# Moving PSUM evacuations and low parts between VectorE, ScalarE and GpSimd in a two-layer diffusion backbone

## Chip, cores and metric

The kernel runs on one core of a Trainium2 chip. The metric is the device time of one execution in microseconds (us); the time given for a kernel is the median of its runs. All times below are us unless marked ns.

## Reference

Two layers of a hybrid backbone work on 512 latent tokens with a prefix of 256 context tokens, 1024 channels wide. Each layer normalises and modulates its input, makes one combined input projection, runs three branches on slices of it (latent attention, a multi-scale pooling mixer, and a bidirectional gated linear attention, GLA), gates and merges them and adds the result to its input:

```python
def trunk_layer(x, xc, mod, mod_c, ...):
    shift, scale, gate = jnp.split(mod[:, None, :], 3, axis=-1)
    z = split_columns((rmsnorm(x, pre_g) * (1 + scale) + shift) @ w_in)
    zc = split_columns((rmsnorm(xc, pre_g) * (1 + scale_c) + shift_c) @ w_in)
    y_mla, yc_mla = mla_branch(z, zc, ...)
    y_pool = pool_branch(z, pool_w, pool_scale)
    y_gla, yc_gla = gla_branch(z, zc, ...)
    out = merge_branches(z, y_mla, y_pool, y_gla, w_bm, w_bp, w_bg, w_out)
    x = x + gate * rmsnorm(out, post_g)
    ...   # the same for the context xc, in the first layer only
```

The GLA runs over chunks of tokens in both directions. Its keys `k` (256 columns of `z`) and values `v` (512 columns) are the two that the change speaks of, and its decays are `log_sigmoid(...) / 16`.

## The kernel before

**Number format.** Everything is float32, and a product of two float32 matrices is made of three TensorE products of rounded parts: `split` (L76 to 78) makes a high part on ScalarE and a low part, value minus high part, on VectorE unless told otherwise; `mm3` (L91 to 94) issues high times high, high times low, low times high.

**Tiles.** The 768 tokens are six tiles `t` of 128: 0 and 1 are context, 2 to 5 the latents. A layer's input is held transposed in two SBUF tensors, `hh` and `hl` (high and low part), as eight blocks `k` of 128 channels by 768 tokens. `z_A` (L304) multiplies a block of weights with it so that the output channels lie on partitions (the keys `gk`, two blocks, each 512 latents and then 256 context tokens); `z_B` (L316) makes tokens by channels (the values `gv`, two weight halves `i` of 256 channels, six tiles each). Their PSUM results leave by way of a staging tile (pool `stage`, two buffers a tag) and a GpSimd DMA to DRAM, from where the GLA scan reads them.

**Who empties PSUM.** `stage_out` (L330 to 339) empties `gk`, `gq` and others, all on ScalarE. `rows_block` (L412 to 418) empties one `gv` tile after another, on ScalarE too; each of the two buffers of PSUM pool `psz` (tag "z") holds one tile of `gv`, so tile t+2 can't be started before tile t has left:

```python
            ps = z_B(blk, w0, w, hT, t, name)
            st = stage.tile([P, w], F32, tag="st", name=f"st_{name}_{t}")
            with urgent():
                act(st, ps)
```

**The input of the second layer.** `emit_hT` (L1099 to 1111) makes it at the end of the first, for two tiles of tokens at a time (three calls of eight blocks, 24 steps). In a step TensorE transposes a block into a PSUM tile `xT` (pool `pst`, tag "t", two buffers); the affine `hv = xT * scale + shift` empties it on VectorE (L1108); ScalarE makes the high part; GpSimd makes the low part, `hl = hv - hh` (L1111, listed at the helper's line, L71). Around it the first layer's output rows `xo` and residuals `xres` are made on VectorE (L74, L294), and the second layer's first weights are split (`wh_gq` on ScalarE, `wl_gq`, `wl_ak` on VectorE).

**The GLA's gates.** `forget(c)` makes the decay of two tiles: matmuls `pre`, then on ScalarE Abs, Exp and Ln, then on VectorE four operations `e <- pre, e`, then Exp on ScalarE. The scan of tile c (`gla_tile`) is a long row of small VectorE multiplications on `pfx`, `sfx` and `tot` with TensorE products `lv` of the operands `pqk` between.

**What sets the order.** No order is written out by hand: the program is built under a scheduler that simulates a time line and puts each engine's instructions in a queue of its own, with `urgent()` raising the priority of what it encloses. Each engine then works through its queue in that order. So an edit of a few lines also moves rows that it doesn't touch.

Of the kernel before, what the change touches and what calls it, by code (L numbers as in the profile page):

```python
# [11 lines left out]
F32 = mybir.dt.float32  # L12
F32R = mybir.dt.float32r
U32 = mybir.dt.uint32
AF = mybir.ActivationFunctionType
ALU = mybir.AluOpType
# [32 lines left out]
def hybrid_kernel(ctx, tc, io, out):  # L49
    nc = tc.nc  # L50
    V, S, G, PE = nc.vector, nc.scalar, nc.gpsimd, nc.tensor

    def opened(name, bufs=2, side=None, space=None):
        kw = {} if space is None else {"space": space}
        return tc.tile_pool(name=name, bufs=bufs, side=side, reuse_waits="tile", **kw)
# [11 lines left out]
    def act(out, in_, func=AF.Copy, **kw):  # L67
        return S.activation(out=out, in_=in_, func=func, **kw)  # L68

    def tt(out, a, b, op=ALU.mult, eng=None):  # L70
        return (eng or V).tensor_tensor(out=out, in0=a, in1=b, op=op)  # L71
# [37 lines left out]
    def urgent(key="x"):  # L109
        return tc.high_priority(offset=offs.get(key, URGENT)) if offs.get(key, URGENT) else nullcontext()  # L110

    def load_split(src, nk, width, name, pool=stream):
        raw = load_raw(src, nk, width, name, pool)
        h = pool.tile([P, nk, width], F32R, tag="wh", name=f"wh_{name}")
        l = pool.tile([P, nk, width], F32R, tag="wl", name=f"wl_{name}")
        with urgent("split"):
            split(h, l, raw)
        return h, l
# [158 lines left out]
    def dtile(shape, name, dt=F32):  # L277
        return dram.tile(shape, dt, name=name)
# [4 lines left out]
    def new_hT(l, pool):  # L283
        return (pool.tile([P, KD, T], F32R, name=f"hh{l}", bufs=1),
                pool.tile([P, KD, T], F32R, name=f"hl{l}", bufs=1))
# [18 lines left out]
    def z_A(blk, hT, with_ctx, name, psum=None, tag="z"):  # L304

        wh, wl = blk
        res = []
        for t0, n in ((CTX, LAT),) + (((0, CTX),) if with_ctx else ()):
            ps = (psum or psz).tile([P, n], F32, tag=tag, name=f"zA_{name}_{t0}")
            for k in range(KD):  # L310
                mm3(ps, wh[:, k, :], wl[:, k, :], hT[0][:, k, t0:t0 + n], hT[1][:, k, t0:t0 + n],
                    k == 0, k == KD - 1)
            res.append((ps, t0, n))
        return res

    def z_B(blk, c0, w, hT, t, name, psum=None, tag="z"):  # L316

        ps = (psum or psz).tile([P, w], F32, tag=tag, name=f"zB_{name}_{t}")
        ts = slice(t * P, t * P + P)
        kb = KD // len(blk)  # L320
        for k in range(KD):
            wh, wl = blk[k // kb]
            mm3(ps, hT[0][:, k, ts], hT[1][:, k, ts], wh[:, k % kb, c0:c0 + w], wl[:, k % kb, c0:c0 + w],
                k == 0, k == KD - 1)
        return ps

    def wblock(l, name, i):
        return load_split(io["w_in"][l, BLOCK_START[name] + i], KD, P, f"{name}{i}_{l}")

    def stage_out(parts, dst, name, scale=None):  # L330

        st = stage.tile([P, T], F32, tag="st", name=f"st_{name}")
        for ps, t0, n in parts:
            if scale is None:
                act(st[:, t0:t0 + n], ps)
            else:
                act(st[:, t0:t0 + n], ps, scale=scale)
        lo = min(p[1] for p in parts)
        nc.gpsimd.dma_start(out=dst[:, lo:T], in_=st[:, lo:T])
# [17 lines left out]
    def layer(l, hT, close_hT, side, todo_mod):  # L357
# [5 lines left out]
        zqk = dtile([8, 64, T], f"zqk{l}")  # L363
# [48 lines left out]
        def rows_block(blk, w0, w, dst, c0, tiles, name):  # L412
            for t in tiles:
                ps = z_B(blk, w0, w, hT, t, name)
                st = stage.tile([P, w], F32, tag="st", name=f"st_{name}_{t}")
                with urgent():
                    act(st, ps)
                nc.gpsimd.dma_start(out=dst[t * P:t * P + P, c0:c0 + w], in_=st)


# [4 lines left out]
        def z_gq():  # L425
            for c in range(2):
                parts = z_A(wblock(l, "gq", c), hT, full, f"gq{c}_{l}", psg, "g")
                stage_out(parts, zqk[2 * c:2 * c + 2].rearrange("a p t -> (a p) t"), f"gq{c}_{l}", scale=0.125)

        def z_gk():  # L430
            for c in range(2):
                parts = z_A(wblock(l, "gk", c), hT, True, f"gk{c}_{l}", psg, "g")
                stage_out(parts, zqk[4 + 2 * c:6 + 2 * c].rearrange("a p t -> (a p) t"), f"gk{c}_{l}")

        w2 = gl.tile([98, GH * P], F32R, tag="w2", name=f"w2_{l}", bufs=1)
        w2raw = gl.tile([98, GH, 2, 64], F32, tag="am", name=f"w2raw{l}")
# [7 lines left out]
        bias = slice(96, 98)  # L444
# [30 lines left out]
        parts = z_A(load_split(io["w_ak"][l], KD, P, f"ak{l}"), hT, True, f"ak_{l}", psg, "g")  # L475
# [10 lines left out]
        for z in (z_gk, lambda: forget(0), z_gq, ) if full else (lambda: forget(0), z_gk):  # L486
            z()
# [4 lines left out]
        f, b = slice(0, 64), slice(64, 128)  # L492
# [152 lines left out]
        for i in range(4):  # L645
            gate_block("gg", i, sg_d["g"], stage_out)
# [12 lines left out]
        c = 1  # L659
        while c in b_next:  # L660
            carry(b, c, b_next)
            c = b_next[c]
# [42 lines left out]
        for g, w in enumerate(WINDOWS):  # L705
# [33 lines left out]
            for t0, n in ((CTX, LAT),) + (((0, CTX),) if full else ()):  # L739
                ps = psg.tile([P, n], F32, tag="g", name=f"pps{l}_{g}_{t0}")  # L740
# [325 lines left out]
        for t in order:  # L1066
            ps = psw.tile([P, 512], F32, tag="w", name=f"wo2_{l}_{t}")
# [31 lines left out]
    def emit_hT(hT, cols, xhs, t0, nt, pool):  # L1099
        st = 1 if t0 < 2 else 0  # L1100
        n = nt * P
        for k in range(KD):
            ps = pst.tile([P, n], F32, tag="t", name=f"xT_{t0}_{k}")
            for i in range(nt):
                PE.transpose(out=ps[:, i * P:i * P + P], in_=xhs[t0 + i][:, k * P:k * P + P], identity=ident)
            at = slice(t0 * P, t0 * P + n)
            v = pool.tile([P, n], F32, tag="hv", name=f"hv_{k}_{t0}", bufs=4)
            V.tensor_scalar(out=v, in0=ps, scalar1=cols[:, 8 + k, st:st + 1], scalar2=cols[:, k, st:st + 1],  # L1108
                            op0=ALU.mult, op1=ALU.add)
            act(hT[0][:, k, at], v)  # L1110
            tt(hT[1][:, k, at], v, hT[0][:, k, at].bitcast(F32), ALU.subtract, G)  # L1111


    gh = ExitStack()
    hT = new_hT(0, gh.enter_context(opened("hT0", 1, "right")))
# [17 lines left out]
    for t in (2, 3, 4, 5, 0, 1):  # L1133
        xh = xhat_tile(xin[t], xin[t], sp, f"x0_{t}")
        for hf in range(2):
            ps = psx.tile([P, 4, P], F32, tag="x", name=f"xT0_{t}_{hf}")
            for i in range(4):
                k = 4 * hf + i
# [14 lines left out]
    for l in range(DEPTH):  # L1153
        hT, close_hT = layer(l, hT, close_hT, side, todo_mod)
# [108 lines left out]
```

## Time and profile before

| what | us |
|---|---|
| median of three runs | 1489.5 |
| lowest, highest of them | 1486.53, 1491.42 |
| the profiled execution | 1493.07 |
| its span (first to last instruction) | 1491.3 |
| outside the span in that execution | 1.77 |
| TensorE matmuls busy | 1440.8 (97% of the span) |
| VectorE busy | 1065.7 (71%) |
| ScalarE busy | 717.6 (48%) |
| GpSimd busy | 516.3 (35%) |

The profile is of one execution. PE is TensorE's matmuls, PEld its weight loads, DVE VectorE, ACT ScalarE, POOL GpSimd. Its views list how long groups of instructions were busy, what an engine was idle before and which other engine's instruction ended that wait, the rows of a stretch in time order, and the busy time in windows, with the clock that TensorE was granted as a share of full speed.

### The profile page before, as it was taken

The numbers are of one execution on the slowest core, as the hardware profiler recorded it, in microseconds if no ns is written. First come the engines' busy times: TensorE is split into PE (matmuls) and PEld (weight loads), VectorE is DVE, ScalarE is ACT, GpSimd is POOL, SyncE is SP. The second block draws the span as 40 slices with busy tenths as digits, with TensorE's granted clock in tenths as the row PEclk, the third lists the DMA queues.
The fourth block names the chain that finished last, engine by engine and source line by source line (L and its number), as shares of the span: only waits on it lengthen the run. The fifth ranks groups of instructions, "written<-read, shape, count | busy, mean of one in ns | idle before, by whom it ended". The sixth has DMA issues, their size and how long they took to land.

```text
span 1491.3 us, 23912 instructions
## 1 busy us (share of the span) xinstructions
PE 1440.8 (97%) x8942; PEld 1275.6 (86%) x8942; DVE 1065.7 (71%) x1980; ACT 717.6 (48%) x1342; POOL 516.3 (35%) x685
## 2 busy tenths in 40 slices
PE   7999999999999999999999988999999999998988
PEld 3799899998888898897889978988978888887878
DVE  3645999957677887877674564699985676677773
ACT  5554453443444445666343347553344555456432
POOL 3431424453313543552111264324652000044530
PEclk9999999999999999999999999999999999999999
DMA  9333333455514334436656144434266323246641
GB/s 363 118 120 121 102 104 97 127 152 183 188 42 154 114 111 128 135 127 210 221 169 207 73 141 125 147 122 139 69 190 225 102 94 104 69 131 191 208 146 57
DMA packets 63875, 209.74 MB, mean 141 GB/s; under 512 B 12120, under 2 KB 15376, under 8 KB 63760
## 3 DMA queue, kind: packets, MB, share of 16 engines
q1 hardware_dynamic: 38688, 116.74, 24.0%
q0 software_dynamic: 24208, 88.34, 18.0%
q10 hardware_dynamic: 864, 3.15, 0.6%
q8 instruction: 70, 1.15, 0.3%
q14 instruction: 45, 0.37, 0.1%
HBM read 161.65 MB, written 46.54 MB: 140 GB/s over the span
## 4 chain that ended last, share of the span: by engine, by line
PE 75%; DVE 12%; issue 4%; DMA 3%; ACT 3%; POOL 3%; ACTq 0%; DVEq 0%; POOLq 0%
PE zA_m L89 20%; PE zB_gv L89 4%; PE sc L89 4%; PE zB_wo L89 4%; PE br_g L89 4%; PE br_m L89 3%; PE zA_pg L89 3%; PE zA_mg L89 3%; PE wo L89 3%; PE av L89 3%; PE br_p L89 3%; PE lv L89 2%; PE pt L860 2%; PE zA_px L89 2%; PE zA_gq L89 2%
## 5 line engine op out<-in xcount | busy, mean ns | idle before, releaser
L89 PE MATMUL zA_m<-hh,wh_m 128*128 128x512 f32 (+1 forms) x576 | 206.4, 358 | 0.0
L89 PE MATMUL zA_m<-hl,wh_m 128*128 128x512 f32 (+1 forms) x576 | 205.7, 357 | 0.0
L89 PE MATMUL zA_m<-hh,wl_m 128*128 128x512 f32 (+1 forms) x576 | 205.3, 357 | 0.0
L89 PEld LDWEIGHTS zA_m<-hh,wh_m 128*128 128x128 f32 x576 | 109.2, 190 | 14.7 <-ACT st_m L68 0.5
L89 PEld LDWEIGHTS zA_m<-hh,wl_m 128*128 128x128 f32 x576 | 108.9, 189 | 14.6 <-DVE wl_m L71 0.4
L89 PEld LDWEIGHTS zA_m<-hl,wh_m 128*128 128x128 f32 x576 | 109.2, 190 | 14.3
L838 DVE TENSOR_REDUCE mx<-sc 128x1 f32<-128x768 f32 (+1 forms) x80 | 67.7, 846 | 46.1 <-PE sc L89 45.2
L68 ACT ACTIVATE pe<-sc,mx 128x768 f32<-128x768 f32 (+1 forms) x80 | 65.2, 815 | 67.5 <-DVE mx L838 67.2
L229 POOL TENSOR_SCALAR raw_mod<-raw_mod,csil 128x256 f32<-128x256 f32 x64 | 70.7, 1108 | 43.1 <-DVE macc L74 17.5
L354 POOL DMA_DIRECT2D sm<-st_m x32 | 17.7, 553 | 190.6 <-ACT st_m L68 181.8
L71 DVE TENSOR_TENSOR wl_m<-raw_m,wh_m 128x1024 fp32r<-128x1024 f32 x48 | 59.1, 1231 | 32.7 <-ACT wh_m L68 31.4
L68 ACT ACTIVATE wh_m<-raw_m 128x1024 fp32r<-128x1024 f32 x48 | 50.8, 1058 | 59.5 <-PE zA_m L89 33.3
L71 DVE TENSOR_TENSOR ptl<-pt,pth 128x256 fp32r<-128x256 f32 (+1 forms) x144 | 72.8, 534 | 8.0 <-ACT pth L68 7.1
L68 ACT ACTIVATE pth<-pt 128x256 fp32r<-128x256 f32 (+1 forms) x144 | 62.7, 474 | 24.9 <-PE pt L860 24.1
L89 PE MATMUL lv<-pqk 128*128 128x128 f32 x560 | 73.4, 275 | 1.3 <-DVE pqk L71 1.2
L89 PEld LDWEIGHTS lv<-pqk 128*128 128x128 f32 x560 | 70.8, 191 | 4.4 <-issue 1.9
L74 DVE SCALAR_TENSOR_TENSOR macc<-raw_mod,csil,macc 128x256 f32<-128x256 f32 x132 | 69.2, 540 | 7.1 <-POOL macc L71 5.4
L71 POOL TENSOR_TENSOR macc<-macc,raw_mod 128x256 f32<-128x256 f32 x64 | 55.8, 873 | 33.9 <-DVE macc L74 21.2
L860 PE MATMUL pt<-ident,pe 128*128 128x128 f32 x416 | 60.8, 273 | 3.2 <-DVE ptl L71 1.7
L89 PE MATMUL zB_gv<-wh_gv,hh 128*128 128x256 f32 x192 | 54.6, 285 | 4.2 <-ACT st_gv L68 2.2
L89 PE MATMUL br_p<-yp,wh_wbp 128*128 128x512 f32 (+1 forms) x192 | 55.4, 370 | 2.6 <-DVE acc L74 1.7
L89 PE MATMUL av<-pth,vv 128*128 128x256 f32 x208 | 55.3, 292 | 2.1 <-ACT pth L68 1.7
(405 smaller groups left out, 4718.9 us busy)
## 6 DMA issues: line engine op xcount, KB each, us to landing
raw_mod<-in_mod_w SPq DMA_DIRECT2D x48, 512.0 KB, 4.6
raw_m<-in_w_in SPq DMA_DIRECT2D x48, 512.0 KB, 4.0
sm<-st_m POOLq DMA_DIRECT2D x24, 384.0 KB, 3.3
raw_wo<-in_w_out SPq DMA_DIRECT2D x16, 512.0 KB, 4.0
sm<-st_m POOLq DMA_DIRECT2D x24, 256.0 KB, 2.5
raw_gv<-in_w_gv SPq DMA_DIRECT2D x8, 512.0 KB, 4.5
raw_gg<-in_w_in SPq DMA_DIRECT2D x8, 512.0 KB, 3.7
raw_px<-in_w_in SPq DMA_DIRECT2D x8, 512.0 KB, 4.2
```

Of the source, the lines that this page charges most:

```text
L68: return S.activation(out=out, in_=in_, func=func, **kw)
L71: return (eng or V).tensor_tensor(out=out, in0=a, in1=b, op=op)
L74: return V.scalar_tensor_tensor(out=out, in0=a, scalar=s, in1=b, op0=op0, op1=op1)
L89: PE.matmul(out=out, lhsT=lhsT, rhs=rhs, start=start, stop=stop)
L229: G.tensor_scalar(out=w, in0=w, scalar1=c, scalar2=None, op0=ALU.mult)
L354: nc.gpsimd.dma_start(out=dst[:, lo:T], in_=st[:, lo:T])
L838: V.tensor_reduce(out=mx, in_=ps[:, 0:nkey], axis=AX.X, op=ALU.max, negate=True)
L860: PE.transpose(out=pt[:, kk, :], in_=pe[:, (k0 + kk) * P:(k0 + kk + 1) * P], identity=ident)
```

## The change

Three places are edited. In `stage_out` an engine can be named, and the second key block (`gk`, c = 1) now leaves PSUM by a VectorE copy, two of them a layer (512 and 256 columns). In `rows_block` the first half of the values (`c0 == 0`) leaves by VectorE copies, six a layer. In `emit_hT` the affine of blocks 2 and 5 goes to ScalarE (6 of 24 steps), and the low part is made on GpSimd for blocks 0, 3 and 6 alone (9 of 24) and on VectorE for the others (15 of 24).

```diff
-    def stage_out(parts, dst, name, scale=None):
+    def stage_out(parts, dst, name, scale=None, eng=None):
         st = stage.tile([P, T], F32, tag="st", name=f"st_{name}")
         for ps, t0, n in parts:
-            if scale is None:
+            if eng is V:
+                V.tensor_copy(out=st[:, t0:t0 + n], in_=ps)
+            elif scale is None:
                 act(st[:, t0:t0 + n], ps)
...
                 with urgent():
-                    act(st, ps)
+                    if c0:
+                        act(st, ps)
+                    else:
+                        V.tensor_copy(out=st, in_=ps)
...
-                stage_out(parts, zqk[4 + 2 * c:6 + 2 * c].rearrange("a p t -> (a p) t"), f"gk{c}_{l}")
+                stage_out(parts, zqk[4 + 2 * c:6 + 2 * c].rearrange("a p t -> (a p) t"), f"gk{c}_{l}", eng=V if c else None)
...
-            V.tensor_scalar(out=v, in0=ps, scalar1=cols[:, 8 + k, st:st + 1], scalar2=cols[:, k, st:st + 1],
-                            op0=ALU.mult, op1=ALU.add)
+            scale, shift = cols[:, 8 + k, st:st + 1], cols[:, k, st:st + 1]
+            if k % 3 == 2:
+                act(v, ps, AF.Identity, scale=scale, bias=shift)
+            else:
+                V.tensor_scalar(out=v, in0=ps, scalar1=scale, scalar2=shift, op0=ALU.mult, op1=ALU.add)
             act(hT[0][:, k, at], v)
-            tt(hT[1][:, k, at], v, hT[0][:, k, at].bitcast(F32), ALU.subtract, G)
+            tt(hT[1][:, k, at], v, hT[0][:, k, at].bitcast(F32), ALU.subtract, G if k % 3 == 0 else V)
```

The scheduler moves other rows along with these. Three places follow; the number behind a name tells one buffer of it from another.

**VectorE, the second layer's input, last two latent tiles.** `hv_4` and `xT_k` belong to tiles 4 and 5 and block k; `xo_0` and `xo_1` are output rows of the first layer. Before:

```order
L71 TENSOR_TENSOR wl_gq_1_9722<-raw_gq_1_9719,wh_gq_1_9721 128x1024
L1108 TENSOR_SCALAR hv_4_9410<-xT_0_9407,mcols_6740 128x256
L1108 TENSOR_SCALAR hv_4_9417<-xT_1_9414,mcols_6740 128x256
L74 SCALAR_TENSOR_TENSOR xo_0_9514<-part_8699,r_post_0_9519,xres_0_9512 128x512
L74 SCALAR_TENSOR_TENSOR xo_0_9514<-xo_0_9514,r_post_0_9519,xres_0_9512 128x512
L71 TENSOR_TENSOR wl_ak_9756<-raw_ak_9753,wh_ak_9755 128x1024
L1108 TENSOR_SCALAR hv_4_9424<-xT_2_9421,mcols_6740 128x256
L1108 TENSOR_SCALAR hv_4_9431<-xT_3_9428,mcols_6740 128x256
```

After the change:

```order
L71 TENSOR_TENSOR wl_gq_1_9722<-raw_gq_1_9719,wh_gq_1_9721 128x1024
L1118 TENSOR_SCALAR hv_4_9410<-xT_0_9407,mcols_6740 128x256
L74 SCALAR_TENSOR_TENSOR xo_0_9514<-part_8699,r_post_0_9519,xres_0_9512 128x512
L74 SCALAR_TENSOR_TENSOR xo_0_9514<-xo_0_9514,r_post_0_9519,xres_0_9512 128x512
L1118 TENSOR_SCALAR hv_4_9417<-xT_1_9414,mcols_6740 128x256
L71 TENSOR_TENSOR wl_ak_9756<-raw_ak_9753,wh_ak_9755 128x1024
L71 TENSOR_TENSOR xo_1_9581<-wo_0_1_9530,pg_1_8697 128x512
L1118 TENSOR_SCALAR hv_4_9431<-xT_3_9428,mcols_6740 128x256
L1118 TENSOR_SCALAR hv_4_9438<-xT_4_9435,mcols_6740 128x256
```

The affine of block 1 now stands behind both operations of `xo_0`, that of block 2 is gone from VectorE, and `wl_ak` no longer stands ahead of it. On TensorE's own queue the transposes of blocks 2 to 5 stood in one run of eight before; now those of blocks 2, 3 and 4 stand so, and 12 matmuls (four of each of two `gq` blocks and of `ak`) come before those of block 5.

**VectorE, the second layer's first values.** `e_0` is the decay of tiles 0 and 1, `st_gk_1` the second key block, `st_gv_1_0` values tile 0 of the first half. Before:

```order
L74 SCALAR_TENSOR_TENSOR e_0_9821<-pre_0_1_9826,e_0_9821 128x256 x2
L71 TENSOR_TENSOR tot_0_9987<-e_0_9821 128x256
L71 TENSOR_TENSOR tot_1_10373<-e_0_9821 128x256
L71 TENSOR_TENSOR tot_0_9991<-tot_0_9987 128x128
L71 TENSOR_TENSOR tot_1_10383<-tot_1_10373 128x128
L71 TENSOR_TENSOR pfx_0_9981<-pfx_0_9981,e_0_9821 128x256
```

After the change:

```order
L74 SCALAR_TENSOR_TENSOR e_0_9821<-pre_0_1_9826,e_0_9821 128x256 x2
L335 COPY st_gk_1_9953<-zA_gk_1_256_9903 128x512
L335 COPY st_gk_1_9953<-zA_gk_1_0_9928 128x256
L71 TENSOR_TENSOR tot_0_9987<-e_0_9821 128x256
L71 TENSOR_TENSOR tot_1_10373<-e_0_9821 128x256
L422 COPY st_gv_1_0_10030<-zB_gv_1_0_10005 128x256
L71 TENSOR_TENSOR tot_0_9991<-tot_0_9987 128x128
L71 TENSOR_TENSOR tot_1_10383<-tot_1_10373 128x128
L71 TENSOR_TENSOR pfx_0_9981<-pfx_0_9981,e_0_9821 128x256
```

The copy of values tile 0 stands behind the two `tot` operations, which read `e_0`. The copy of tile 1 comes 11 rows after it, that of tile 2 12 rows later, that of tile 3 13 rows later with the four operations `e_2 <- pre_2` among these, that of tile 4 after one row more, that of tile 5 after another 11.

**ScalarE, the same place.** Before:

```order
L68 ACTIVATE st_gk_1_9953<-zA_gk_1_256_9903 128x512
L68 ACTIVATE st_gk_1_9953<-zA_gk_1_0_9928 128x256
L68 ACTIVATE st_gv_1_0_10030<-zB_gv_1_0_10005 128x256
L68 ACT_TABLE_LOAD
L68 ACTIVATE e_0_9821<-e_0_9821 128x1024
L68 ACTIVATE pfx_0_9981<-e_0_9821,masks 128x512
L68 ACTIVATE sfx_0_9982<-e_0_9821,masks 128x512
L68 ACTIVATE pfx_1_10367<-e_0_9821,masks 128x512
L68 ACTIVATE sfx_1_10368<-e_0_9821,masks 128x512
L68 ACTIVATE st_gv_1_1_10058<-zB_gv_1_1_10033 128x256
L68 ACTIVATE st_gv_1_2_10086<-zB_gv_1_2_10061 128x256
```

After the change:

```order
L68 ACTIVATE e_0_9821<-e_0_9821 128x1024
L68 ACT_TABLE_LOAD
L68 ACTIVATE e_0_9821<-e_0_9821 128x1024
L68 ACTIVATE pfx_0_9981<-e_0_9821,masks 128x512
L68 ACTIVATE sfx_0_9982<-e_0_9821,masks 128x512
L68 ACTIVATE pfx_1_10367<-e_0_9821,masks 128x512
L68 ACTIVATE sfx_1_10368<-e_0_9821,masks 128x512
L68 ACTIVATE e_2_10400<-pre_2_0_10401 128x2x2x128
L68 ACTIVATE e_2_10400<-pre_2_1_10405 128x2x2x128
```

The last Exp of `e_0` (the row behind the table load) stood behind three evacuations and now follows the row before it directly; the values tiles 1 and 2, which stood behind four affines of the scan, have left this queue.

## Rows read from the trace of the kernel before

**Rows 1.** The page: busy time of each engine, share, instructions.

```profile
PE 1440.8 (97%) x8942; PEld 1275.6 (86%) x8942; DVE 1065.7 (71%) x1980; ACT 717.6 (48%) x1342; POOL 516.3 (35%) x685
```

**Rows 2.** TensorE's waits, waiting group and releaser: sum us, count, longest.

```profile
PE xT L1105 <- DVE hv L1108: 4.2, 2, 3.5
PE pre L89 <- DVE e L74: 2.5, 2, 2.3
PE zB_gv L89 <- ACT st_gv L68: 2.2, 1, 2.2
```

**Rows 3.** TensorE's timeline, 866 to 930: start, duration, instruction, [idle before, releaser].

```profile
871.09 1.14 PE L1105 MATMUL xT<-ident,xres 128*128 128x128 f32 x4 [3.48 <-DVE hv L1108]
...
921.35 0.28 PE L89 MATMUL zB_gv<-wh_gv,hh 128*128 128x256 f32 x1
...
926.61 0.38 PE L89 MATMUL zB_gv<-wh_gv,hh 128*128 128x256 f32 x1 [2.23 <-ACT st_gv L68]
```

**Rows 4.** VectorE's timeline, 864 to 872.

```profile
864.83 1.38 DVE L71 TENSOR_TENSOR wl_gq<-raw_gq,wh_gq 128x1024 fp32r<-128x1024 f32 x1 [0.30 <-ACT wh_gq L68]
866.13 0.98 DVE L1108 TENSOR_SCALAR hv<-xT,mcols 128x256 f32<-128x256 f32 x2
...
867.70 1.21 DVE L74 SCALAR_TENSOR_TENSOR xo<-xo,r_post,xres 128x512 f32<-128x512 f32 x1
868.83 1.75 DVE L71 TENSOR_TENSOR wl_ak<-raw_ak,wh_ak 128x1024 fp32r<-128x1024 f32 x1
870.50 0.98 DVE L1108 TENSOR_SCALAR hv<-xT,mcols 128x256 f32<-128x256 f32 x2
```

**Rows 5.** All instructions on tile hv: least/mean/most ns, first and last start, shapes.

```profile
L1108 DVE TENSOR_SCALAR hv<-xT,mcols x24: 527/533/544, 851.6 to 899.5; 128x256 f32<-128x256 f32 x24
...
L71 POOL TENSOR_TENSOR hl<-hv,hh x24: 731/743/1793, 853.8 to 900.8; 128x256 fp32r<-128x256 f32 x24
L71 DVE TENSOR_TENSOR hl<-hv,hh x16: 409/608/695, 31.1 to 60.6; 128x512 fp32r<-128x512 f32 x8, 128x256 fp32r<-128x256 f32 x8
```

**Rows 6.** ScalarE's timeline: two affines with a scale and a bias column.

```profile
936.84 1.13 ACT L68 ACTIVATE pqk<-e,masks,masks 128x256 f32<-128x256 f32 x2
```

**Rows 7.** Windows: length; busy us (count) PE PEld DVE ACT POOL; clock; DMA share; GB/s.

```profile
865.70:871.40 5.70, 1.50 (x9) 0.71 (x7) 5.70 (x8) 3.62 (x9) 4.35 (x5) 1.00 0.87 303
871.40:874.80 3.40, 3.38 (x11) 2.68 (x10) 3.40 (x7) 0.97 (x3) 2.98 (x3) 0.50 0.47 159
```

**Rows 8.** All instructions on tile st_gv.

```profile
L68 ACT ACTIVATE st_gv<-zB_gv x24: 360/385/388, 95.8 to 953.3; 128x256 f32<-128x256 f32 x24
```

**Rows 9.** ScalarE's timeline, 920 to 924.

```profile
920.97 1.28 ACT L68 ACT_TABLE_LOAD   x1 [0.49 <-DVE e L74]
922.26 1.06 ACT L68 ACTIVATE e<-e 128x1024 f32<-128x1024 f32 x1
```

**Rows 10.** VectorE's timeline, 923 to 934.

```profile
923.36 0.76 DVE L71 TENSOR_TENSOR tot<-e 128x256 f32<-128x256 f32 x2 [2.46 <-ACT e L68]
924.03 0.49 DVE L71 TENSOR_TENSOR tot<-tot 128x128 f32<-128x128 f32 x2
...
926.92 0.26 DVE L71 TENSOR_TENSOR tot<-tot 128x16 f32<-128x16 f32 x2
...
932.13 1.42 DVE L74 SCALAR_TENSOR_TENSOR e<-pre,e 128x256 f32<-128x256 f32 x4
```

**Rows 11.** Windows of the second layer's values and scan, columns as in rows 7.

```profile
926.70:930.00 3.30, 3.30 (x28) 3.30 (x29) 3.30 (x14) 2.52 (x5) 1.11 (x2) 1.00 0.38 132
947.30:953.00 5.70, 5.70 (x50) 5.70 (x49) 0.29 (x4) 1.83 (x3) 1.62 (x3) 1.00 0.45 137
953.00:960.00 7.00, 7.00 (x40) 6.00 (x39) 4.56 (x3) 2.75 (x4) 4.02 (x3) 1.00 0.50 170
1050.00:1100.00 50.00, 46.48 (x307) 42.66 (x306) 46.88 (x93) 21.86 (x53) 33.16 (x42) 1.00 0.33 98
```

**Rows 12.** VectorE's timeline in the first layer, at its keys and values.

```profile
101.21 0.69 DVE L71 TENSOR_TENSOR pqk<-pfx,up 128x512 f32<-128x512 f32 x1 [6.00 <-DMA up<-zqk]
```

## Prediction

> **What bounds the kernel.** I read the page's busy times first: TensorE's matmuls fill 97% of the span, and VectorE, the next, 71% [rows 1]. A change that gives TensorE nothing less to do can only shorten the time by shortening TensorE's waits, or lengthen it by adding to them. So next I read which waits TensorE has where the edited rows run. There are three [rows 2]: the transposes `xT` of the second layer's input wait 4.2 for VectorE's affines; the gate matmuls `pre` wait 2.5 for VectorE, the longest 2.3; the values' matmuls `zB_gv` wait once, 2.2, for ScalarE. TensorE's timeline puts them in the second layer's opening, 866 to 927 [rows 3]. The reader is to see there that less than 9 us of 1491 are within the change's reach, and that each wait is one for a PSUM buffer that another engine has still to empty.
>
> **The new layer's input: a gain.** The longest of the `xT` waits, 3.48, ends at 871.09 [rows 3]. VectorE's rows say why: behind the affines of blocks 0 and 1 (0.98 for both, from 866.13) stand the two `xo` operations and then `wl_ak` of 1.75, and only at 870.50 come the affines of blocks 2 and 3 [rows 4], whose PSUM buffers blocks 4 and 5 need. After the change VectorE makes block 0 (0.45, the step from one affine to the next: 0.98 less one affine's 0.53 [rows 4, 5]), then `xo_0` twice, which took from 867.11 (866.13 + 0.98) to 868.83, 1.72, then block 1. That is 866.13 + 0.45 + 1.72 = 868.30, and block 1 is out at 868.83. Block 2 goes to ScalarE meanwhile: an affine with two column operands takes 0.56 there (1.13 for two [rows 6]), and ScalarE was busy 3.62 of the 5.70 here [rows 7], so block 2 is out before block 1. Block 3's transposes are released at 868.8, block 4's before that, and block 5's have 12 matmuls ahead of them, which cover the affine of block 3 behind `wl_ak`. The last wait ends at 868.8 in place of 871.09: **−2.3**. Its bounds are 0 (a wait for a low part takes its place) and −4.2 (both `xT` waits go [rows 2]).
>
> A low part takes GpSimd 0.743 and VectorE, in the first layer's input, 0.409 at the least [rows 5]. The 15 that move take VectorE 15 × 0.41 = 6.2 to 15 × 0.74 = 11.2, less 6 × 0.53 = 3.2 for the affines that go. They come in three bursts of eight blocks, of which this one, with the last latent tiles, is where TensorE has nothing else to do; in it VectorE was full (5.70 of 5.70 [rows 7]), and what is put on it moves `wl_ak` and later weights. I cost that at nothing, because the 12 matmuls on block 0 cover the low parts of the next blocks; without that cover the 5 low parts of this burst cost TensorE 5 × 0.41 = 2.1, which takes back nearly all of the gain, and is inside the bound of 0 above.
>
> One row of VectorE stands out. The second `xo` took 1.21, where the first took 0.6 from start to start (867.11 to 867.70), and GpSimd was at work for 4.35 of the 5.70 around it [rows 4, 7]. [...]
>
> **The gate matmuls: nearly nothing.** `pre` of tiles 2 and 3 waits for the decay of tiles 0 and 1, which VectorE ends after two ScalarE functions. ScalarE's queue changes by one evacuation's worth there: between 0 and 0.39 [rows 8], and I take **+0.2**.
>
> **The second layer's first values: a loss.** A tile of values is 24 matmuls at 3.30/28 = 0.118 [rows 11], so 2.8. It can't start until the tile two before has left its PSUM buffer. Before, ScalarE did that at 0.385 a tile [rows 8], and TensorE waited 2.23 once, when two evacuations stood behind a table load, the Exp and four affines on ScalarE [rows 3, 9]. Now VectorE does it. What a copy of 128x256 from PSUM takes there no row shows; the nearest are ScalarE's at 0.36 to 0.388 [rows 8] and VectorE's affine from PSUM at 0.53 [rows 5]. I take 0.45, the affine's step from start to start, as it is the same engine, source and size. [...]
>
> The price of a copy matters less than where it stands. In the queue the first copy is behind the two `tot` operations, and these wait for ScalarE's Exp, which ends at 923.3 [rows 9]; they ran from 923.36 to 924.03 [rows 10]. (Without the evacuations the Exp hardly comes earlier: the table load starts when VectorE's `e` is done.) So:
> - tile 0 is out at 924.03 + 0.45 = 924.5; tile 2 was ready to start at 921.35 [rows 3]: wait 3.1.
> - 11 rows follow, those which ran from 924.03 to 926.92 before bar one of 0.33, so 2.55; tile 1 is out at 924.48 + 2.55 + 0.45 = 927.5, while tile 2 ends at 924.5 + 2.8 = 927.3: wait 0.2.
> - 12 rows follow, 3.04 by their steps; tile 2 is out at 931.0, tile 3 ends at 930.3: wait 0.65.
> - 13 rows follow, 4.56, of which the four `e` take 1.42 [rows 10]; tile 3 is out at 936.0, tile 4 ends at 933.8: wait 2.2.
> - tile 4 is one row behind and tile 5 has its matmuls ahead: no wait.
>
> Together 6.15 in place of 2.23: **+3.9**. Bounds: +3.2, if copies cost 0.36 and VectorE's rows close up a little; +5.1, if the `e` of the next decay stall the queue for ScalarE as the first did (2.46 [rows 10]) and half of that shows. The stores of these tiles go out from GpSimd behind each copy as they did before, one a tile, and GpSimd, busy 35% [rows 1], is relieved by 15 × 0.743 = 11.1 at the layer's opening; the scan reads no value before all six tiles are through.
>
> **The other copies: nothing.** In the first layer VectorE idles 6.00 before 101.21, where keys and values leave [rows 12]. In the second, the second key block's copies stand ahead of the `tot` in VectorE's wait of 2.46 for the Exp [rows 10]. ScalarE, which is relieved of 16 evacuations, about 16 × 0.385 = 6, and given six affines of 0.56, is busy 48% [rows 1] and sets no wait here but those named. If the cover were gone the eight of a layer would cost VectorE 8 × 0.45 = 3.6.
>
> **Sum.** −2.3 + 0.2 + 3.9 = **+1.8**. The profiled execution took 1493.07, of which 1491.3 is the span; that is 3.57 above the median of the runs. +1.8 makes it 1494.9, and on the median 1489.5 it is **1491.3**. A difference of 0.3%, 4.5 us, is about what a measurement of this kernel can tell from no change: 1485.0 and 1494.0 are the bounds.
>
> **Rivals.**
> 1. *The boundary clears entirely (faster).* Both `xT` waits go, −4.2 rather than −2.3. [...] And as the first products of the scan now stand some 6 us of work earlier in TensorE's queue, its late waits (50.00 − 46.48 = 3.5 idle in 1050 to 1100 [rows 11]) shrink by 3. That is 1.8 − 1.9 − 1.7 − 3.0 = −4.8, so **1484.7**. For it: VectorE is the only thing that ends those waits. Against it: my walk leaves a wait of over 1 us at block 3, and the clock didn't fall after the 2.23 wait [rows 3, 11], so idle alone doesn't foretell it. Chance 0.30.
> 2. *The second layer's scan becomes VectorE's (slower).* In 1050 to 1100 VectorE is busy 46.88 of 50, more than TensorE's 46.48 [rows 11]. The copies of the second layer come ahead of the scan's rows; if VectorE has no slack left to make up for them, the scan ends 8 × 0.45 = 3.6 later; and if the 3.1 wait at the values is followed by a stretch at half clock like that at 871.4, 1.7 more. 1.8 + 3.6 + 1.7 = +7.1, so **1496.6**. It decides where VectorE has less than 3.6 of idle between the copies and the scan's end. Against it: 5.4 idle in 947.3 to 953 and 2.4 in the next 7 [rows 11]. Chance 0.25.
> 3. *Gain and loss cancel or both are absent:* the scheduler's order elsewhere moves waits about, and the time is within 2 us of 1489.5. It lies in the forecast's own range.
>
> **How the numbers follow.** My forecast, the gain at the transposes given back at the values' copies, has 0.45, and is 1491.3 with an own range from 1487 (the values at +3.2, the boundary at −4.2 and the clock's 1.7 saved: −2.5) to 1495 (no gain at the boundary and the values at +5.1: +5.3). The range reaches past both rivals by the spread of the runs before, some 2.5 either way, cut where 2 in 10 are left out: 1482 to 1498. Faster than 1485.0 is rival 1 alone: 0.30. Slower than 1494.0 is rival 2 and a tail of the forecast of 0.03: 0.28. The rest, 0.42, is no difference.
>
> **What would show it.** Right: TensorE's wait at `xT` ends near 868.8 and sums to about 2; its waits at `zB_gv` name VectorE's copy, two of them over 2 us, and sum to about 6; `wl_ak` ends earlier relative to the transposes; VectorE's copy from PSUM lasts 0.4 to 0.55. Wrong: a `zA_gq` wait for a low part in place of the `xT` waits; the `zB_gv` waits under 3, which would mean that the queue doesn't hold the copies as I walked it; the window after the boundary at clock 1.00; more than 3.5 idle in the late scan.

## The result, and the profile after

The changed kernel takes 1500.66 (median of 5, 1498.53 to 1503.49) where the kernel before took 1491.42 (median of 5): the ratio is 1.0064, with a 95% interval of 1.0047 to 1.0081. It is slower, by about 9.2, and lies above the range of the prediction. The profiled execution took 1501.1, with a span of 1499.3, 8.0 longer than the span of the one before; the rows below are of these two.

The page of the changed kernel, busy times, to set beside [rows 1]:

```profile
PE 1443.3 (96%) x8942; PEld 1280.1 (85%) x8942; DVE 1076.4 (72%) x2005; ACT 712.9 (48%) x1332; POOL 500.6 (33%) x670
```

No engine has become the bound. VectorE has 10.7 more to do and is at 72%. So the time went into waits and clock: TensorE's same 8942 matmuls are busy 2.5 longer (1443.3 against 1440.8), and TensorE idles 5.5 longer (56.0 against 50.5), together the 8.0. Some of TensorE's waits of the changed kernel, as in [rows 2]:

```profile
PE sc L89 <- ACT pe L68: 6.5, 8, 1.5
...
PE kps L89 <- ACT klh L68: 4.7, 1, 4.7
PE zA_m L89 <- ACT wh_m L68: 3.1, 2, 2.1
PE zB_gv L89 <- DVE st_gv L422: 3.0, 1, 3.0
PE pre L89 <- DVE e L74: 2.6, 2, 2.4
...
PE xT L1110 <- DVE hv L1118: 1.7, 2, 1.1
...
PE xT L1110 <- ACT hv L68: 0.7, 1, 0.7
```

The last four of these are the places that the prediction spoke of. The waits `kps` and `zA_m` for these releasers have no counterpart before; both lie in the **first** layer, in its attention, 250 us and more after the edited rows there. The wait `sc`, in the attention of both layers, was 2.5 before. Windows over the stages (columns as in rows 7) show what they are worth. Before:

```profile
375.00:420.00 45.00, 45.00 (x269) 39.82 (x269) 24.71 (x43) 20.10 (x36) 12.62 (x18) 1.00 0.49 160
420.00:730.00 310.00, 306.57 (x1925) 271.64 (x1924) 244.76 (x504) 167.29 (x357) 125.52 (x143) 0.99 0.42 138
...
900.00:945.00 45.00, 40.23 (x309) 38.65 (x309) 29.39 (x77) 35.58 (x55) 22.57 (x40) 1.00 0.47 141
```

And the changed kernel:

```profile
375.00:420.00 45.00, 39.49 (x216) 34.51 (x215) 23.00 (x38) 17.56 (x30) 14.45 (x19) 0.92 0.50 165
420.00:730.00 310.00, 301.70 (x1901) 269.88 (x1900) 240.93 (x493) 162.22 (x352) 120.58 (x141) 0.98 0.39 126
...
398.70:405.50 6.80, 5.33 (x22) 4.73 (x23) 5.66 (x8) 4.74 (x9) 0.00 (x0) 0.50 0.14 47
...
900.00:945.00 45.00, 39.38 (x253) 36.31 (x252) 25.36 (x62) 29.02 (x44) 18.07 (x32) 0.92 0.44 138
```

In 375 to 420 TensorE was never idle before and now is for 5.5, and runs 6.8 of the rest at a granted clock of 0.50: 53 matmul rows fewer get through. The wait of 4.7 and half of the 5.33 that it was busy at that clock make about 7.4, an estimate from these rows. In 420 to 730 it idles 8.3 instead of 3.4. In 900 to 945, around the second layer's keys and values, the clock is 0.92 instead of 1.00; but there the changed kernel is more than 10 us behind in its work, so the two rows don't hold the same matmuls.

One milestone splits the loss by layer: the start of the first affine of the second layer's input. Instructions on tile hv (the middle figure is the median, as it is in [rows 5] and [rows 8]):

```profile
L1118 DVE TENSOR_SCALAR hv<-xT,mcols x18: 531/536/546, 865.0 to 912.3; 128x256 f32<-128x256 f32 x18
...
L68 ACT ACTIVATE hv<-xT,mcols x6: 546/564/565, 867.8 to 908.3; 128x256 f32<-128x256 f32 x6
```

It started at 851.6 before [rows 5] and at 865.0 now, with 5400 of TensorE's matmuls started ahead of it in both. The first layer is 13.4 longer; the second, 1491.3 − 851.6 = 639.7 before, is 1499.3 − 865.0 = 634.3 now, 5.4 shorter. The prediction had the whole effect in the second layer and none in the first.

**Where the first layer lost it.** ScalarE's timeline at the first attention's start, before and after the change:

```profile
392.86 0.26 ACT L68 ACTIVATE wh_wk<-raw_wk 128x64 fp32r<-128x64 f32 x1 [3.69 <-DMA raw_wk<-in_w_k]
...
393.60 0.42 ACT L68 ACTIVATE wh_wq<-raw_wq 128x256 fp32r<-128x256 f32 x1 [0.22 <-DMA raw_wq<-in_w_uq]
394.26 0.94 ACT L68 ACTIVATE klh<-lat,kn 128x768 fp32r<-128x768 f32 x1 [0.24 <-DMA lat<-latents]
```

```profile
396.18 0.26 ACT L68 ACTIVATE wh_wk<-raw_wk 128x64 fp32r<-128x64 f32 x1 [5.99 <-DMA raw_wk<-in_w_k]
398.87 0.42 ACT L68 ACTIVATE wh_wq<-raw_wq 128x256 fp32r<-128x256 f32 x1 [2.44 <-DMA raw_wq<-in_w_uq]
399.19 0.92 ACT L68 ACTIVATE klh<-lat,kn 128x768 fp32r<-128x768 f32 x1
```

`klh`, the keys' latents, which the first product `kps` needs, stands behind the split of the first query weights, and that waits for its load. TensorE's cover of `zA_m` ends at 395.4 either way. The DMA queue of SyncE in the same two kernels:

```profile
383.13 3.79 SPq L106 DMA_DIRECT2D raw_mod<-in_mod_w  x2
387.02 0.55 SPq L106 DMA_DIRECT2D raw_wk<-in_w_k  x1
387.62 0.51 SPq L106 DMA_DIRECT2D raw_wq<-in_w_uq  x1
```

```profile
384.80 2.81 SPq L106 DMA_DIRECT2D raw_mod<-in_mod_w  x2
387.71 1.14 SPq L106 DMA_DIRECT2D raw_wk<-in_w_k  x1
388.90 0.52 SPq L106 DMA_DIRECT2D raw_wq<-in_w_uq  x1
```

In both, the load of the query weights stands behind two loads `raw_mod` of 512 KB. It is issued 1.3 later now and lands 9.9 after its issue where it took 6.0, so 5.2 later; most of that is the longer transfer. Nothing here was edited. What the edit did was to move the scheduler's order: in the two traces TensorE's matmuls stand in another order from the 590th on, through the first layer's scan, pooling and attention.

The longer one of the `zA_m` waits, 2.1, ends at 651.5. ScalarE's split of that weight block had stood for its load, too:

```profile
650.38 1.06 ACT L68 ACTIVATE wh_m<-raw_m 128x1024 fp32r<-128x1024 f32 x1 [2.53 <-DMA raw_m<-in_w_in]
```

No experiment takes this second place apart.

**At the places that the prediction walked.** VectorE's timeline of the changed kernel, at the transposes of the last two tiles and at the second layer's values:

```profile
880.07 0.53 DVE L1118 TENSOR_SCALAR hv<-xT,mcols 128x256 f32<-128x256 f32 x1
880.53 0.74 DVE L74 SCALAR_TENSOR_TENSOR xo<-part,r_post,xres 128x512 f32<-128x512 f32 x1
881.18 1.22 DVE L74 SCALAR_TENSOR_TENSOR xo<-xo,r_post,xres 128x512 f32<-128x512 f32 x1
882.33 0.53 DVE L1118 TENSOR_SCALAR hv<-xT,mcols 128x256 f32<-128x256 f32 x1
...
932.68 1.01 DVE L335 COPY st_gk<-zA_gk 128x512 f32<-128x512 f32 x2
935.22 0.76 DVE L71 TENSOR_TENSOR tot<-e 128x256 f32<-128x256 f32 x2 [1.53 <-ACT e L68]
935.90 0.42 DVE L422 COPY st_gv<-zB_gv 128x256 f32<-128x256 f32 x1
```

The rows stand as walked: the affine of block 1 behind the two `xo`, and the first values copy behind the two `tot`, which wait for ScalarE's Exp.

### The profile page after: what moved, and what is told of

Read it like the earlier page. It is cut to its first block, busy times and chain, and to the rows that moved or that the text cites. A ratio compares the mean times of both kernels' runs of the same rounds, so it can differ in the third digit from the quotient of the medians.

```text
span 1499.3 us, 23919 instructions
## 1 busy us (share of the span) xinstructions
PE 1443.3 (96%) x8942; PEld 1280.1 (85%) x8942; DVE 1076.4 (72%) x2005; ACT 712.9 (48%) x1332; POOL 500.6 (33%) x670
## 4 chain that ended last, share of the span: by engine, by line
PE 63%; issue 14%; DVE 12%; DMA 5%; POOL 3%; ACT 3%; POOLq 0%; ACTq 0%; DVEq 0%
PE zA_m L89 10%; PE zB_gv L89 5%; PE zB_wo L89 4%; PE br_g L89 4%; PE zA_pg L89 4%; PE br_m L89 3%; PE zA_mg L89 3%; PE lv L89 3%; PE wo L89 3%; PE sc L89 2%; PE zA_gk L89 2%; PE zB_qkv L89 2%; PE zA_gg L89 2%; PE zA_gq L89 2%; PE br_p L89 2%
## 5 line engine op out<-in xcount | busy, mean ns | idle before, releaser
L865 PEld LDWEIGHTS pt<-ident,pe 128*128 128x128 f32 x416 | 49.7, 142 | 7.9 <-ACT pe L68 1.0
L89 PE MATMUL sc<-kth,qth 96*128 96x256 f32 (+1 forms) x144 | 50.1, 348 | 6.5 <-ACT pe L68 6.5
```

What stands on the lines that cost most here:

```text
L89: PE.matmul(out=out, lhsT=lhsT, rhs=rhs, start=start, stop=stop)
L865: PE.transpose(out=pt[:, kk, :], in_=pe[:, (k0 + kk) * P:(k0 + kk + 1) * P], identity=ident)
```

## The experiments

The theory: the loss comes from the first layer, where the copies of the values moved the scheduler's order, and not from work that an engine has more of. The rival: VectorE's added work is the loss, at the boundary, or in the copies themselves. All ratios are to runs of the kernel before on the same chip; "first affine" is the start of VectorE's first `hv` of the second layer's input in the profiled execution (851.6 before, 865.0 changed).

**The input edit alone** (input_only below).

```diff
-                    if c0:
-                        act(st, ps)
-                    else:
-                        V.tensor_copy(out=st, in_=ps)
+                    act(st, ps)
...
-                stage_out(parts, ..., f"gk{c}_{l}", eng=V if c else None)
+                stage_out(parts, ..., f"gk{c}_{l}")
```

> The input edit alone (affines of blocks 2 and 5 on ScalarE, 15 of 24 low parts on VectorE); all keys and values leave by ScalarE as before, and TensorE's queue is that of before up to the boundary. Theory (the loss comes from the first layer, where the copies of the values moved the scheduler's order): about 2 us faster than before, as the waits at the transposes fall from 4.4 to about 2.7, and no wait of over 1 us for klh near 395. Rival (the loss comes from what VectorE has to do at and after the boundary): slower than before by 5 or more.

Measured: 1.0015 (0.9996 to 1.0033), first affine at 850.2, no wait for `klh`. The transposes wait 2.3 (1.6 for VectorE, 0.7 for ScalarE) instead of 4.2. But the gain doesn't arrive, and the wait at the values is longer with every evacuation still on ScalarE:

```profile
PE zB_gv L89 <- ACT st_gv L68: 4.4, 1, 4.4
```

ScalarE's timeline of this kernel shows why: with the low parts moved, the scheduler put the first values evacuation behind the Exp and three affines of the scan; before, it stood ahead of that Exp.

```profile
919.25 1.06 ACT L68 ACTIVATE e<-e 128x1024 f32<-128x1024 f32 x1
...
922.47 0.36 ACT L68 ACTIVATE st_gv<-zB_gv 128x256 f32<-128x256 f32 x1
```

It is neither the theory's 2 faster nor the rival's 5 slower. The rival falls.

**Copies in the second layer only, with the input edit.**

```diff
-                    if c0:
+                    if c0 or full:
...
-                stage_out(..., eng=V if c else None)
+                stage_out(..., eng=V if c and not full else None)
```

> The input edit, and VectorE copies of keys and values in the second layer only; the first layer's queues are those of before. Theory: within 3 us of before (transposes -2, values of the second layer +3, a few us of waits moved about in the second layer's scan and attention). Rival: 7 to 10 us slower than before, as the whole change is.

Measured: 0.9981 (0.9963 to 0.9999), first affine at 853.5. The time is as the theory said. The waits at `zB_gv` are 3.6 for VectorE, of which 3.0 is the first copy.

**Copies in the first layer only.** The mirror of it (`if c0 or not full`, `eng=V if c and full else None`), with all affines on VectorE and all low parts on GpSimd again.

> VectorE copies of keys and values in the first layer only; the input edit and the second layer's copies are undone. Theory: at least 8 us slower than before, with the wait for klh of over 4 near 397, granted clock 0.50 behind it, and the longer waits of the first attention (sc for ACT pe, zA_m for ACT wh_m), as in the changed kernel. Rival: no slower than 2 us; the wait for klh was an accident of one execution.

Measured: 1.0055 (1.0039 to 1.0071), first affine at 865.4, a wait of 4.2 for `klh` and 3.7 at `zA_m`. The whole loss is in this part. The wait is no accident of one execution.

**The same copies, other tiles.** That first-layer copies cost could still be their work. Two kernels part work from order. In one, the other half of the values leaves by VectorE in the first layer:

```diff
-                    if c0:
+                    if (not c0 if full else c0):
                         act(st, ps)
```

> The whole change, but in the first layer it is the second half of the values (i = 1) that leaves by VectorE, and the first half by ScalarE: the same six copies, the same load on every engine. TensorE's queue in the first layer is then nearly that of before (16 of some 4400 rows stand elsewhere). Theory (the order costs, not the copies): no wait of over 1 us for klh near 395, and the time of the kernel with copies in the second layer only, 0 to 4 us under before. Rival (VectorE's six copies in the first layer cost): about 9 over before, as the whole change.

In the other, only half as many copies move:

```diff
-                    if c0:
+                    if c0 or (full and t < 3):
                         act(st, ps)
```

> The whole change, but in the first layer only tiles 3, 4 and 5 of the first half leave by VectorE, tiles 0 to 2 by ScalarE: half of the copies, and TensorE's queue is row for row that of the whole change. Theory (the order costs): 8 to 10 over before, with the wait for klh of over 4 near 397. Rival (the copies cost): half of the loss, 4 to 5 over before.

Measured: 0.9994 (0.9983 to 1.0005) with six copies of the second half, first affine at 850.3, and 1.0053 (1.0039 to 1.0068) with three copies of the first half, first affine at 864.2. Windows of the second half's kernel, then of the three copies':

```profile
375.00:420.00 45.00, 45.00 (x269) 39.89 (x268) 25.17 (x43) 20.08 (x35) 12.30 (x17) 1.00 0.50 163
420.00:730.00 310.00, 306.87 (x1943) 273.06 (x1943) 245.53 (x505) 168.49 (x360) 124.14 (x143) 1.00 0.41 139
```

```profile
375.00:420.00 45.00, 39.48 (x216) 34.42 (x215) 22.00 (x37) 17.58 (x30) 13.48 (x18) 0.92 0.50 164
```

In the traces, the second half's kernel has TensorE's order of before in the first layer but for some ten of 5400 matmuls; the three copies' kernel has the changed kernel's order throughout. Six copies with the old order cost nothing in the first layer; three copies with the new order cost all of it. So the order is the cause, and the number of copies is not; a kernel with the new order and no copies was not run. (The median of the second half's kernel lay 1.4 under before, inside the interval; I had expected 0 to 4.)

**Inside the first layer: the query weights' split out of the way.**

```diff
-            wqh, wql = load_split(io["w_uq"][l, head], 2, P, f"wq{l}_{head}", ap)
+            wqh, wql = load_split(..., ap, hi=G if full and head == 0 else None)
...
-            split(h, l, raw)
+            if hi is None:
+                split(h, l, raw)
+            else:
+                hi.tensor_copy(out=h, in_=raw)
+                tt(l, raw, h.bitcast(F32), ALU.subtract, hi)
```

> The changed kernel with one thing more: the query weights of the first layer's head 0 (wh_wq, wl_wq) are split by GpSimd, so that klh on ScalarE and kll on VectorE don't stand behind rows which wait for that load. All other rows stand as in the changed kernel. Theory: the wait of 4.7 at kps falls to 2.5 or less, the clock stays at 1.00 there, and the time is 4 to 7 us under the changed kernel's (3 to 6 over before). Rival (the load is late because the DMA engines are full, and lat is as late as raw_wq): the wait stays over 4 and the time as it was, 9 over before.

Measured: 1.0036 (1.0019 to 1.0053). The wait at `kps` fell to 2.9, not under 2.5, and the clock stayed at 1.00 there; first affine at 860.4. So the place behind the split is worth about 2 of the 4.7, and the time is some 4 under the changed kernel's, as the theory had it, though the two intervals overlap a little. The key weights' own load came late as well in this execution (`wh_wk` at 398.11), and `kps` reads these weights too.

**Without the 512 KB loads ahead.**

```diff
-                if full and n_mod >= 6 and n_mod % 6 != 3:
+                if full and n_mod >= 8 and n_mod % 6 != 3:
                     next(todo_mod, None)
```

> The whole change, with the chunks of the next layer's modulation started two gate blocks later, so that no 512 KB load of them is issued just ahead of the first head's weights; TensorE's queue is that of the whole change up to 100 rows before kps. Theory (klh waits because its load and raw_wq share full DMA engines with two raw_mod loads): the wait for klh falls from 4.7 to under 2 and the clock stays at 1.00 after it. Rival (the loads are late because their buffers come free late): the wait stays over 4. The time of the whole kernel decides nothing here, as later rows move too; 4 to 9 over before.

Measured: no wait at `kps`, clock 1.00. SyncE's queue and ScalarE's `klh` in this kernel:

```profile
376.09 0.33 SPq L106 DMA_DIRECT2D raw_wk<-in_w_k  x1
376.47 0.48 SPq L106 DMA_DIRECT2D raw_wq<-in_w_uq  x1
```

```profile
390.33 0.94 ACT L68 ACTIVATE klh<-lat,kn 128x768 fp32r<-128x768 f32 x1 [0.92 <-DMA lat<-latents]
```

The loads go out 12 earlier, which speaks against buffers that come free late. This run takes away two things at once, the late issue behind `raw_mod` and the company of its loads on the DMA engines (mean busy share 0.92 to 1.05 from 388 to 397 in the changed kernel). Two kernels nearly part them: `raw_wq` is issued at 388.08 in the input edit alone and at 388.90 in the changed kernel, 0.8 later, and lands 5.8 after that in the one and 9.9 in the other, where `klh` is waited for. So it is for the most part the longer transfer and not the issue. What makes the transfer longer when the same two loads stand ahead of it in both is open. The time, 1.0157 (1.0132 to 1.0182), is worse than I expected: the modulation's later chunks are then late, and TensorE waits 3.6 at `modt` for their sums and 4.0 at the products `br_g`.

**The second layer: the affines apart from the low parts.**

```diff
-            tt(hT[1][:, k, at], v, hT[0][:, k, at].bitcast(F32), ALU.subtract, G if k % 3 == 0 else V)
+            tt(hT[1][:, k, at], v, hT[0][:, k, at].bitcast(F32), ALU.subtract, G)
```

together with copies in the second layer only (affines_layer2 below).

> Copies of keys and values by VectorE in the second layer only, and of the input edit the affines alone (blocks 2 and 5 on ScalarE; all low parts on GpSimd). In VectorE's queue the first copy of the second layer's values then stands ahead of the two tot. Theory (the 3.1 wait at zB_gv is the copy's place behind tot): that wait falls under 0.6, and the time is 2 to 4 under that of the kernel with copies in the second layer and the whole input edit, 4 to 7 under before. Rival (the wait goes to a later copy: that of tile 3 stands 16 rows behind that of tile 2): a wait of 2 to 3 there, and the time 1 to 3 under before.

Measured: 0.9975 (0.9959 to 0.9990). The first copy's wait fell to 0.4 as the theory had it, and a wait of 2.0 for the copy of tile 3 came in, as the rival had it; together 2.4. The transposes wait 4.0 (3.4 and 0.6). The time is 3.7 under before, between what the theory and the rival expected; against the kernel with the whole input edit and the same copies (0.9981) the intervals overlap, so a lead over that one is not shown.

**The affines alone.** The same edit, with keys and values by ScalarE in both layers.

> Of the whole change the affines of blocks 2 and 5 on ScalarE alone; all low parts on GpSimd, all keys and values by ScalarE. On ScalarE the first values evacuation then stands ahead of the last Exp of e_0 as before, while with the low parts moved too it stands behind it. Theory (the low parts' move costs the 4.4 wait at zB_gv of input_only by that place): the zB_gv wait for ScalarE is 2.2 as before, the waits at the transposes 3.4 for VectorE and 0.6 for ScalarE as in affines_values, and the time is within 2 of before. Rival (the affines on ScalarE push that evacuation back): a zB_gv wait of over 4, and 2 to 3 over before.

Measured: 1.0002 (0.9987 to 1.0017). The transposes wait 3.4 and 0.6 as expected, `zB_gv` 2.7 for ScalarE rather than 2.2, and not 4.4: it is the low parts' move that pushes the evacuation back. The affines gain 0.2 of the 4.2 at the transposes, as much as the same wait differs between two executions without the input edit (4.2 and 4.4); most of the 1.8 that the whole edit gains there comes with the low parts.

**Copies in the second layer, without the input edit.** All affines on VectorE, all low parts on GpSimd (layer2_alone below).

> Copies of keys and values by VectorE in the second layer only, and no input edit. The first copy of the values stands ahead of the two tot here too. Theory: the waits at the transposes are those of before (about 4.4), the wait for the first copy is under 0.6; 1 to 3 under before. Rival (the copies in the second layer cost what the walk said): 3 to 4 over before.

Measured: 0.9988 (0.9977 to 0.9998); the transposes wait 4.2, the values' matmuls 2.5 for VectorE, none over 2.1. The walk's +3.9 for the copies doesn't hold where the first one stands ahead of `tot`.

**Values without keys.** First with the affines on ScalarE (affines_values), then alone; the diff to affines_layer2 and to layer2_alone is one line.

```diff
-                stage_out(..., eng=V if c and not full else None)
+                stage_out(...)
```

> As affines_layer2, but the second key block leaves by ScalarE in both layers: VectorE copies of six values tiles in the second layer, and affines of blocks 2 and 5 on ScalarE. The copy of values tile 3 then stands ahead of the four e_2 rows. Theory (that copy's wait of 2.0 came from the e_2 ahead of it): the zB_gv waits for VectorE fall from 2.4 to under 1, and the time is 0 to 3 under affines_layer2, 4 to 7 under before. Rival (the wait is 23 rows long either way, and the order of the second layer's attention, which also changes, decides): 2 to 4 over affines_layer2.

> VectorE copies of the six values tiles of the second layer alone; no input edit, no key copies. Theory: transposes wait 4.2 as before, zB_gv waits for VectorE under 2.5, and the time is 1 to 3 under before. Rival (the second layer's copies are a loss of 3.9 as the walk said): 3 to 4 over before.

Measured: 0.9945 (0.9929 to 0.9962), a median of 1479.85 against 1488.49, for the first: the best of all. 0.9980 (0.9967 to 0.9993) for the second, with 1.9 at `zB_gv` and 4.2 at the transposes, as expected. In the best kernel, TensorE's waits in the second layer's opening, and the window of the values:

```profile
PE xT L1110 <- DVE hv L1118: 3.4, 2, 2.5
PE zB_gv L89 <- DVE st_gv L422: 2.5, 2, 1.4
PE pre L89 <- DVE e L74: 2.2, 2, 2.0
```

```profile
900.00:945.00 45.00, 40.31 (x309) 38.59 (x308) 33.61 (x88) 30.79 (x43) 19.99 (x34) 1.00 0.47 145
```

My reason for it falls: the waits at `zB_gv` are 2.5 as they were 2.4, only cut into 1.1 and 1.4. The clock is 1.00 over this window where affines_layer2 has 0.92, but over the whole execution the mean granted clock is 0.992 in both. Of the 5.3 between the two spans, 2.4 lies in the first layer, which is the same in both kernels, TensorE's order too; that part is no work of the edit. The rest of the lead over affines_layer2 I can't lay to a single step: the order of the second layer's attention changes too, which was the rival.

## Why the prediction was wrong

- **The step that failed** is "The other copies: nothing." The copies themselves did cost nothing in the first layer, as it says: six with the old order leave the time at 0.9994. But the step priced a copy where it stands, by VectorE's idle time, and took the order around it as given, although the text on the kernel says that the scheduler sets it. Moving them moved TensorE's order from its 590th matmul on, and that cost 13.4 in the first layer. So the premise of the whole sum, that less than 9 us are within the change's reach, was wrong too: it counted the waits at the edited rows alone. The third rival had it ("the scheduler's order elsewhere moves waits about") and bounded it by 2 us with no row behind that bound.
- *The transposes, −2.3:* right in mechanism, a little large. The waits are 2.4 in place of 4.2, so −1.8. The walk had block 1 out 2.7 after block 0 began; VectorE's rows give 882.86 − 880.07 = 2.8.
- *The gate matmuls, +0.2:* 2.6 in place of 2.5.
- *The values, +3.9:* the first wait, 3.1 by the walk, is 3.0, and it is the only one; two of over 2 and a sum of about 6 had been forecast. The later ones (0.2, 0.65, 2.2) don't show in the changed kernel, as TensorE ran at half clock just then, and the copies were in time for it. The window 934.5 to 941.4:

```profile
934.50:941.40 6.90, 5.03 (x23) 5.03 (x24) 6.18 (x25) 4.93 (x8) 3.61 (x7) 0.51 0.51 169
```

  With 0.8 more wait (3.0 in place of 2.2) and half of the 5.03 at that clock, 2.5, the stage lost about 3.3, an estimate from these rows: near the 3.9, but for the most part by the clock, which the forecast had in a rival and not in the sum. Where the copy stands ahead of `tot`, about 2 of wait appears at tile 3, as the walk had it.
- *The walked part as a whole, +1.8:* from the first affine to the last values evacuation it was 953.3 − 851.6 = 101.7 before [rows 5, 8] and is 968.4 − 865.0 = 103.4 now, +1.7. That it fits so well is in part luck, as the clock stood in for the later waits.

```profile
L422 DVE COPY st_gv<-zB_gv x12: 409/418/425, 94.6 to 953.0; 128x256 f32<-128x256 f32 x12
L68 ACT ACTIVATE st_gv<-zB_gv x12: 383/383/385, 114.8 to 968.4; 128x256 f32<-128x256 f32 x12
```

- *A copy of 128x256 from PSUM:* taken at 0.45; 0.418 in the median of 12, 0.33 from start to start.
- *Rivals.* The second, slower, had the right sign for a wrong reason: the loss is in the first layer, and VectorE is not the scan's bound (46.18 of 50 in 1050 to 1100, against 46.88 [rows 11], while TensorE went from 46.48 to 47.74; the same clock times, not the same work). The first, faster, is right in sign for kernels without the first layer's copies and the low parts' move, but not in mechanism: the transposes still wait 4.0 in them. No run shows the 1.7 that this rival's sum and the forecast's range take off for the clock: the kernel before had a clock of 0.50 for 3.4 behind its transposes' waits [rows 7], and the changed kernel, with the waits at 2.4, had 0.51 for 3.4, from 883.3 to 886.7.
- *Not foreseen:* the second layer got 5.4 shorter although its walked part got 1.7 longer, so some 7 came behind the values. That is no work of the edits there: the kernel with copies in the first layer alone, whose second layer is not edited, is 7.2 shorter in it (1497.9 − 865.4 = 632.5). From the last values evacuation to the end it takes 528.0 and the changed kernel 530.9, with TensorE's order there nearly the same in both; the three kernels without any VectorE copies (before, the input edit alone, the affines alone) take 535.1 to 538.0. Copies in either layer change the scheduler's order there as well; which rows of it gain was not taken apart.

The median of the five runs of before is 1491.42, 1.9 above the one that the prediction started from; that changes no sign.

## What to carry to other kernels

Where a scheduler sets the order, an edit's cost has two parts: what the moved rows cost at their place, which the trace of before tells well, and what the new order does elsewhere, which it doesn't tell at all. Before predicting, compare the two orders on the busiest engine over the whole program and give each region that moved a bound from its nearest waits, in both directions; then split a mixed change by region, since here the parts that lost 13 and won 5 were hidden in one figure, and a part that is not edited can move too. A useful control is the same work with another choice of tiles that leaves the order alone.

## What the runs showed that I had not expected

- After nearly the same wait at the second layer's values the granted clock fell in one kernel and not in another. With a wait of 2.2 it stayed at 1.00 before [rows 3, 11]; in the kernel with copies in the first layer alone, with a wait of 2.1 there for the same evacuation by ScalarE, it was 0.50 for 6.8, of which TensorE was busy 5.70. In both, the gate matmuls had waited shortly before, 2.3 and 2.4. In the best kernel it stayed at 1.00 after a wait of 2.0 at `pre` and one of 1.1 at the values. So what the clock adds to a wait of 2, here between nothing and 5.70 / 2 = 2.9, can't be told from the wait alone.
- The first layer's length to the first affine varied from 846.6 to 853.5 over nine executions in which its order was, but for a few rows, that of before, and from 864.2 to 865.4 over three with the new order and nothing added. Differences of 2 or 3 us between two profiles say nothing without several runs.
- The second `xo` still takes 1.22 where the prediction looked, but the traces say more than the one row that it had. One tile later it took 1.22 before and takes 0.74 now: before, three low parts ran on GpSimd beside it; now GpSimd does nothing there from 887.8 to 891.4. VectorE before, GpSimd before, VectorE after:

```profile
875.78 1.22 DVE L74 SCALAR_TENSOR_TENSOR xo<-xo,r_post,xres 128x512 f32<-128x512 f32 x1
```

```profile
873.52 4.09 POOL L71 TENSOR_TENSOR hl<-hv,hh 128x256 fp32r<-128x256 f32 x3
```

```profile
889.44 0.74 DVE L74 SCALAR_TENSOR_TENSOR xo<-xo,r_post,xres 128x512 f32<-128x512 f32 x1
```

  Of the twenty such rows in the two traces, the five beside a low part on GpSimd take 1208 to 1225 ns and the fifteen others 741 to 749 ns. In these two the first `xo` of a pair takes 735 to 765 ns with and without a low part beside it, so being beside one is not enough to be slowed; in the kernel with the affines alone one first `xo` took 1.22 too (at 855.48). What decides it the traces don't show. At 881.18 in the changed kernel a single low part of 0.72 stands beside the 1.22.
